# A two-layer encoder step: the first down product's weight sums moved from the feed-forward into the attention's second half

## The chip, the cores and the metric

The kernel runs on one core of a Trainium2 chip. The metric is the device time of one execution in microseconds (us). A measurement is the median of several runs. The engines are TensorE (PE, matrix products), VectorE (DVE), ScalarE (ACT), GpSimd (POOL) and SyncE (SP, which here only issues transfers).

## The reference

One inference step of a hybrid encoder with two layers, all in float32, on 1024 prompt positions and 64 sample positions (1088 together). The first layer mixes by windowed attention, the second by a complex diagonal state-space model (SSM). After each mixer comes a convolutional feed-forward:

```python
def conv_ffn(h, prev, w_up, conv_w, conv_b, w_down):
    up = h @ w_up                                   # 1024 -> 2 x 2816
    full = jnp.concatenate([prev.astype(up.dtype), up], axis=1)
    c = conv_b
    for j in range(CONV_WIDTH):                     # 3
        c = c + conv_w[j] * full[:, j:j + t]
    y = (jax.nn.gelu(c[..., :D_FF]) * c[..., D_FF:]) @ w_down   # 2816 -> 1024
    return y, full[:, -(CONV_WIDTH - 1):]
...
for i in range(DEPTH):
    mp, ... = attn_prompt(rms_norm(xp, ...), ...)   # layer 0; s5_mixer in layer 1
    xp = xp + rms_norm(mp, g_post_mix[i])
    fp, cpi = conv_ffn(rms_norm(xp, g_pre_ffn[i]), ...)
    xp = xp + rms_norm(fp, g_post_ffn[i])
```

## The kernel before

Every product is made in three fp32r matmuls of a split operand (`mm3`, L223 to L225): high weight by low activation, high by high, low by high. Weights come by `load_unit`: SyncE loads a tile `raw` (two buffers), ScalarE and VectorE split it into `whl` (L216; L193/L194 for parts of the down product). Tokens go in three blocks of 384, 384 and 320.

The stages follow one another: normalization, attention, output projection, first feed-forward, SSM, gated unit, second feed-forward.

**The attention.** `staged` (a helper) runs 34 units `scores(c, p)`, one for each chunk and half of the heads, three at a time in a pipeline: the scores (L772), maxima (L778) and exponentials (L783); the scaling (L791) and the transposes (L795); the product with the values (L802). Beside each unit it takes one step of a generator `beside()`. Its first 15 steps make the rest of K and Q, step 16 stores keys, and the next 20 make the output projection (`go`, L223 to L225, evicted at L839 and L857). So the second half of the heads runs beside the projection. At the end come the normalizations: `post_norm` (L317 to L331) and `pre_norm` (L300 to L308), which makes `hh` and `hl`, the two parts of the feed-forward's input.

**The feed-forward.** For each of 22 gate tiles, `up` makes two tiles of the up product (evicted by VectorE at L414/L416), `conv` the convolution (L422 to L424), and `gate` the gated product (L440), which SyncE stores to `gd` (L441). Twice in each gate tile, `aside()` takes a step of `ssm_prep()`, at lower priority, which prepares the SSM's matrices: first some hundred small VectorE operations (`ssm_small`), then eight chunks with matmuls `kps` (L1069), copies `kt` (L1074), transposes `wps` (L1080) and GpSimd tables `tab`.

**The down product.** For the two full blocks it is a product by Strassen's scheme in Winograd's form: seven products in place of eight, four of which read sums of weights and four sums of gate outputs. `aside()` also calls `sums(j)`, which starts and finishes these sums by a timetable `starts`: at odd steps 1 to 21 `sums_w(k)`, one for each of eleven pairs of weight tiles, and at even steps 24 to 44 `sums_g(k)` for the gate outputs. `sums_w(k)` loads 1 MB of `w_down` into `jt` (L355, SyncE), makes four VectorE operations of 128x512 in place (L358 to L361) and stores the four sums to `sd` in memory (L362, SyncE), one step later. `jt` is one tile of 12 KB per partition, taken from the pool slot `ypA` that also holds `y`, the feed-forward's output; `sums_w` uses its first 8 KB and `sums_g` (L367 to L377) its two halves in turn. The second feed-forward does the same on GpSimd's queue in a buffer `jw` of its own.

The order of instructions on each engine is made by a list scheduler that goes by priority (the order of the program) and its own cost model; `later` and `order` bend it. GpSimd's transfers take their descriptors from a scratch in SBUF, whose size is set where the program is made; before, that is the default.

Of the kernel before, what the change touches and what calls it, by code (L numbers as in the profile page):

```python
# [2 lines left out]

# [5 lines left out]
F32 = mybir.dt.float32  # L9
# [6 lines left out]
P = 128  # L16
# [10 lines left out]
SIDE = 32  # L27

PLAIN = 5

KCUT = (0, 12, 22)
GT = [[(4, "blkA")] * 3, [(4, "blkB"), (4, "blkB"), (2, "big")]]
# [2 lines left out]
KH = KF // 2  # L35
# [8 lines left out]
class Core:  # L44
    def __init__(self, ctx, tc, a):
        self.ctx, self.tc, self.nc, self.a = ctx, tc, tc.nc, a
        nc = self.nc
        pool = lambda n, **k: ctx.enter_context(tc.tile_pool(name=n, bufs=1, **k))
        self.ready, self.wsrc = [], [("w_qk", 8), ("w_qk", 0), ("w_qk", 1), ("w_v", 0), ("w_v", 1)] + [("w_qk", m) for m in (2, 3, 9, 4, 5, 6, 7)]
        self.wsrc += [("w_o", m) for m in range(KD)]  # L50
        for i in range(2):
            for m in range(KF):
                sums = [("w_sum", m, e) for e in (1, 0)] if i == 1 and m >= PLAIN else []
                self.wsrc += [("w_up", i, m)] + sums + [("w_up", i, m + KF)]
            self.wsrc += [("w_part", i, k) + x[:3] for x in PRODUCTS for k in range(0, KH, 2)]
            self.wsrc += [("w_down", i, k, mh) for c in range(2) for mh in range(2) for k in range(KCUT[c], KCUT[c + 1], 2)]
            if i == 0:
                self.wsrc.append(None)
                self.wsrc.append(None)
                self.wsrc += [("w_glu", m + e) for m in range(KD) for e in (0, KD)]  # L60
        self.const = pool("const")
        self.wts = pool("wts")
        self.blk = pool("blk")
        self.yp = pool("yp")
        self.tmp = pool("tmp")
        self.small = pool("small")
        self.open_ps()
        self.dram = pool("dr", space=bass.MemoryType.DRAM)
        jp = self.col_minus_row()
        self.ident = self.const.tile([P, P], F32, name="ident")  # L70
        nc.vector.tensor_scalar(self.ident, jp, 0.0, None, op0=ALU.is_equal)
        self.ones = self.const.tile([P, 1], F32, name="ones")
        nc.vector.memset(self.ones, 1.0 / D)
        self.eps = self.const.tile([P, 1], F32, name="eps")
        nc.vector.memset(self.eps, 1e-6)
        nc.scalar.activation(self.const.tile([P, 1], F32, name="warm"), self.eps, AF.Copy)
        pp = a["pp"]
        self.pp = self.const.tile([P, pp.shape[1]], F32, name="ppt")
        nc.sync.dma_start(self.pp[:, :64], pp[:, :64])
# [141 lines left out]
    def mm3(self, out, w, sl, xh, xl, start, stop, more=False):  # L221
# [2 lines left out]
        nc.tensor.matmul(out, w[:, 0, sl], xh, start=False, stop=False, skip_group_check=more)  # L224
        self.last_mm = nc.tensor.matmul(out, w[:, 1, sl], xh, start=False, stop=stop, skip_group_check=more)  # L225

    def fill(self, ps, n, cols, first=None):

        for _ in range(n):
            x = self.nc.tensor.matmul(ps[:, :cols], self.ident, self.pp[:, 64:64 + cols] if cols > P else self.ident[:, :cols], start=True, stop=True)  # L230
            if first is not None:
                self.order(x, first)
            first = x
        return x
# [105 lines left out]
    def ffn(self, i, h, rb, after, side=None, beside=lambda: None, x=None, g=None):  # L340

        nc, tc, a = self.nc, self.tc, self.a
# [2 lines left out]
        cb = lambda m: self.pp[:, off["cb"] + i * 44 + m:off["cb"] + i * 44 + m + 1]  # L345
        cst = self.small.tile([P, 44, 2, 2], F32, name="cst", bufs=1)
        gd = self.dram.tile([P, KF, T], F32, name=f"gd{i}")
        sd = self.sd = self.dram.tile([P, KH, 2, 2, 512], F32, name=f"sd{i}")
        td = self.dram.tile([P, KH, 2, 2, 384], F32, name=f"td{i}")

        E, Q = nc.vector, (nc.sync, nc.gpsimd)[i]

        def sums_w(k):
            x = (jt[:, :2048] if i == 0 else self.yp.tile([P, 2048], F32, name="jw", tag="ypB", bufs=1)).rearrange("p (c h m) -> p c h m", c=2, h=2)
            Q.dma_start(x, a["w_down"][i, k::KH].rearrange("c p (h m) -> p c h m", h=2))  # L355
            yield
            a11, a12, a21, a22 = x[:, 0, 0], x[:, 1, 0], x[:, 0, 1], x[:, 1, 1]
            E.tensor_add(a22, a21, a22)  # L358
            E.tensor_sub(a21, a11, a21)
            E.tensor_sub(a11, a22, a11)  # L360
            E.tensor_sub(a12, a12, a11)  # L361
            Q.dma_start(sd[:, k], x)  # L362

        def sums_g(k):
            x = jt[:, k % 2 * 1536:k % 2 * 1536 + 1536] if i == 0 else ts.tile([P, 1536], F32, name="jg", tag="t2")
            x = x.rearrange("p (c b t) -> p c b t", c=2, b=2)
            Q.dma_start(x, gd[:, k::KH, :768].rearrange("p c (b t) -> p c b t", b=2))  # L367
            yield
            a11, a12, a21, a22 = x[:, 0, 0], x[:, 0, 1], x[:, 1, 0], x[:, 1, 1]
            v = E.tensor_sub(a11, a12, a11)  # L370
            if i == 1:

                self.order(v, self.last_conv)
            E.tensor_sub(a12, a22, a12)
            E.tensor_sub(a22, a22, a11)
            E.tensor_sub(a21, a21, a22)
            Q.dma_start(td[:, k], x)  # L377


        w0 = (PLAIN + 1) * i  # L380
        starts = {2 * (k + w0) + 1: sums_w(k) for k in range(KH)}
        starts.update({2 * (k + KH) + 2: sums_g(k) for k in range(KH)})
        jobs = {}

# [42 lines left out]
        def up(ms):  # L427

            wu = {m: up_start(m) for m in ms}
            for b in range(3):  # L430
                for w, u in wu.values():
                    up_block(w, u, b)
            return {m: u for m, (w, u) in wu.items()}

        def gate(f, us):
            ta = conv(f, us.pop(f) if f in us else up([f])[f])
            nc.scalar.activation(ta, ta, AF.Gelu_apprx_tanh)
            aside()
            tb = conv(KF + f, us.pop(KF + f) if KF + f in us else up([KF + f])[KF + f])
            nc.vector.tensor_mul(ta, ta, tb)  # L440
            Q.dma_start(gd[:, f, :SEQ], ta[:, :SEQ])  # L441
            Q.dma_start(gd[:, f, SEQ:], ta[:, SEQ + 2:])
# [19 lines left out]
        def normed(bs):  # L462

            for b in bs:
                t0, n = BLK[b]
                for k in range(KD):
                    v = nc.vector.scalar_tensor_tensor(x[b][:, k], x[b][:, k], g[:, k:k + 1], rb[:, t0:t0 + n], op0=ALU.mult, op1=ALU.mult)
                    self.order(v, self.last_conv)

        def input_sums():  # L470

            V = nc.vector
            b11, b21, b12, b22 = (half(x[b], j) for b in range(2) for j in range(2))
            t1, t4 = (self.big([P, 4, 384], "t", F32) for _ in range(2))
            t2 = ts.tile([P, 4, 384], F32, name="t2", tag="t2")
            for o, u, v in ((t1, b12, b11), (b12, b22, b12), (t2, b22, t1), (t4, b21, t2)):
                for k in (slice(0, 2), slice(2, 4)):
                    self.order(V.tensor_sub(o[:, k], u[:, k], v[:, k]), self.last_conv)
            op["t1"] = [ts.tile([P, 4, 384], F32R, name=f"t1{j}") for j in range(2)]
            split(*op["t1"], t1)  # L480
            return t2, t4
# [42 lines left out]

        us = up([0, KF, 1])
        gate(0, us)
        if i == 0:
            jt = self.yp.tile([P, 3072], F32, name="jt", tag="ypA", bufs=2)
        else:
            ts_ctx = tc.tile_pool(name="ts", bufs=1)  # L530
            ts = ts_ctx.__enter__()
            op = {}
        aside()
        for f in range(1, KF):
            if i == 1 and f == 2:
                normed((0, 1))
            if i == 1 and f == 3:
                late = input_sums()
            if i == 1 and f == PLAIN - 1:
                us = up([f, KF + f])  # L540
                into_place(*late)
                normed((2,))
            if i == 1 and f >= PLAIN:
                us = seven(f, f == PLAIN)
                if f == PLAIN:
                    for j in range(2):
# [126 lines left out]
    def attention(self, h, rb, after):  # L673
        nc, tc, a = self.nc, self.tc, self.a
        off = PPO
        with tc.tile_pool(name="at", bufs=1) as ap:
# [40 lines left out]
            for tt in range(9):  # L717
# [9 lines left out]
                i = tt - 3 * b  # L727
# [135 lines left out]
            def beside():  # L863
                yield from rest()
                for p in range(2):
                    nc.gpsimd.dma_start(a["o_kp"][:, p], kT[:, p, SEQ - P:SEQ])
                    nc.gpsimd.dma_start(a["o_ks"][:, p, :64], kT[:, p, T + 64:])
                    nc.gpsimd.dma_start(a["o_ks"][:, p, 64:], kT[:, p, SEQ:T])
                yield
                yield from half()  # L870
            self.staged([scores(c, p) for p in range(2) for c in range(17)], beside())
        with self.boundary():
            for m, b in self.tail_order(KD, 4):
                if m >= 4 or b == 2:
# [732 lines left out]
```

## Time and profile before

| | us |
|---|---|
| median of 3 runs | 2242.29 (2237.78 to 2243.76) |
| the profiled execution's own time | 2249.18 |
| its span, first to last instruction | 2247.4 |
| output projection beside the scores | 207 to 314 |
| first feed-forward's gate tiles | 385 to 900 |
| `sums_w`, first operation to last | 399 to 571 |
| `sums_g` of the first feed-forward | 685 to 958 |
| granted TensorE clock, mean | 0.990 |

The profile is one execution. "Busy" is the time in which an engine executes; a matmul's end is modelled, so TensorE reads as busy while matmuls follow one another. A row of the timeline gives start, duration, engine, line, operation, output from inputs, and in brackets the idle time before it with what ended it. In the table by stretches, the number in brackets is a count of instructions.

### The profile page before, as it was taken

Reading aid. Unit: us, or ns where it says so; the run is one execution under the profiler, and the core shown is the slowest. Engines: PE = TensorE matmul, PEld = TensorE weight load, DVE = VectorE, ACT = ScalarE, POOL = GpSimd, SP = SyncE. Lnnn points to the kernel's source line nnn. Section 1 sums busy time; section 2 is a strip of 40 time slices with the busy share of each in tenths; the row PEclk is TensorE's granted clock in tenths of the full one; section 3 lists DMA queues with packets and bytes.
Section 4 is the critical chain, followed back from the end, with each engine's and each line's share of the span. In section 5 each row is a group of like instructions: output and inputs, shape, how many; then the busy total and the mean of one; then the engine's idle time right before and its main releaser. Section 6 shows DMA issues by size and latency. Waiting matters only on the chain.

```text
span 2247.4 us, 35994 instructions
## 1 busy us (share of the span) xinstructions
PE 2194.5 (98%) x13875; PEld 2121.5 (94%) x13875; DVE 1659.1 (74%) x2886; ACT 1044.5 (46%) x1890; POOL 413.9 (18%) x474
## 2 busy tenths in 40 slices
PE   9999999999999999999998899999999999999997
PEld 8987789899999999999996799999999999999997
DVE  8687648989877777667768865687977776676764
ACT  5256746422333343455534742253455445455543
POOL 5322004200042423000200034352011110110000
PEclk9999999999999999999999999999999999999999
DMA  5100015655345565887649988751266676578773
GB/s 196 37 22 29 20 62 162 239 187 207 112 136 190 174 206 176 265 292 221 224 147 339 285 277 291 266 167 65 88 213 240 235 276 224 204 264 311 223 254 99
DMA packets 208123, 428.47 MB, mean 191 GB/s; under 512 B 23312, under 2 KB 114224, under 8 KB 205008
## 3 DMA queue, kind: packets, MB, share of 16 engines
q1 hardware_dynamic: 175648, 326.56, 44.0%
q0 software_dynamic: 23984, 95.12, 11.8%
q10 hardware_dynamic: 8320, 4.49, 0.8%
q8 instruction: 109, 1.79, 0.3%
q14 instruction: 62, 0.51, 0.1%
HBM read 297.75 MB, written 128.37 MB: 190 GB/s over the span
## 4 chain that ended last, share of the span: by engine, by line
PE 45%; DMA 8%; DVE 5%; issue 2%; ACT 1%; POOL 1%; SPq 1%; DVEq 0%; ACTq 0%; POOLq 0%
PE mm L223 14%; PE mm L225 14%; PE mm L224 14%; DMA sj<-in_w_up 3%; DMA yd<-ys 1%; DMA raw<-in_w_down 1%; DMA su<-sj 1%; DMA yf<-yd 1%; DVE whl L216 1%; DMA pm<-prm 0%; DMA hd<-xs 0%; POOL sj L1389 0%; DVE wk L1304 0%; PE pr L266 0%; DMA raw<-in_w_glu 0%
## 5 line engine op out<-in xcount | busy, mean ns | idle before, releaser
L223 PE MATMUL mm<-hl,whl 128*128 128x384 f32 (+1 forms) x1960 | 643.3, 329 | 5.8 <-DVE hl L306 3.1
L224 PE MATMUL mm<-hh,whl 128*128 128x384 f32 (+1 forms) x1960 | 642.8, 328 | 0.0
L225 PE MATMUL mm<-hh,whl 128*128 128x384 f32 (+1 forms) x1960 | 640.2, 328 | 1.9 <-DVE whl L216 1.9
L223 PEld LDWEIGHTS mm<-hl,whl 128*128 128x128 f32 x1960 | 368.9, 188 | 7.6 <-DVE hl L306 4.1
L225 PEld LDWEIGHTS mm<-hh,whl 128*128 128x128 f32 x1960 | 368.6, 188 | 2.3 <-DVE whl L216 2.2
L224 PEld LDWEIGHTS mm<-hh,whl 128*128 128x128 f32 x1960 | 369.1, 188 | 0.0
L216 DVE TENSOR_TENSOR whl<-raw,whl 128x1024 fp32r<-128x1024 f32 x202 | 257.4, 1276 | 148.2 <-ACT whl L216 147.7
L216 ACT ACTIVATE whl<-raw 128x1024 fp32r<-128x1024 f32 x202 | 212.9, 1058 | 271.2 <-PE mm L225 153.9
L223 PE MATMUL mm<-gt,whl 128*128 128x384 f32 (+1 forms) x968 | 317.7, 328 | 1.4 <-ACT whl L216 1.4
L225 PE MATMUL mm<-gt,whl 128*128 128x384 f32 (+1 forms) x968 | 316.7, 328 | 0.7 <-DVE whl L216 0.7
L224 PE MATMUL mm<-gt,whl 128*128 128x384 f32 (+1 forms) x968 | 317.0, 328 | 0.0
L223 PEld LDWEIGHTS mm<-gt,whl 128*128 128x128 f32 x968 | 182.9, 189 | 1.7 <-ACT whl L216 1.7
L225 PEld LDWEIGHTS mm<-gt,whl 128*128 128x128 f32 x968 | 182.7, 189 | 1.0 <-DVE whl L216 1.0
L224 PEld LDWEIGHTS mm<-gt,whl 128*128 128x128 f32 x968 | 182.8, 189 | 0.0
L194 DVE TENSOR_TENSOR whl<-raw,whl 128x1024 fp32r<-128x1024 f32 x84 | 96.4, 1154 | 67.5 <-ACT whl L193 67.1
L193 ACT ACTIVATE whl<-raw 128x1024 fp32r<-128x1024 f32 x84 | 82.7, 988 | 107.1 <-DMA raw<-sd 46.8
L423 DVE SCALAR_TENSOR_TENSOR t<-u,ppt,t 128x1090 f32<-128x1090 f32 x88 | 123.6, 1406 | 7.4 <-ACT t L422 5.8
L424 DVE SCALAR_TENSOR_TENSOR t<-u,ppt,t 128x1090 f32<-128x1090 f32 x88 | 123.5, 1403 | 0.4
L422 ACT ACTIVATE t<-u,ppt 128x1090 f32<-128x1090 f32 x88 | 114.1, 1297 | 12.7 <-DVE t L424 5.4
L563 DVE TENSOR_TENSOR gt<-gr,gt 128x768 fp32r<-128x768 f32 (+2 forms) x106 | 90.3, 881 | 14.7 <-ACT gt L562 14.0
L562 ACT ACTIVATE gt<-gr 128x768 fp32r<-128x768 f32 (+2 forms) x106 | 78.4, 773 | 42.1 <-DMA gr<-gd 29.3
L414 DVE TENSOR_TENSOR u<-rb,mm 128x384 f32<-128x384 f32 (+1 forms) x164 | 80.4, 502 | 20.4 <-PE mm L225 15.4
(389 smaller groups left out, 4105.9 us busy)
## 6 DMA issues: line engine op xcount, KB each, us to landing
raw<-in_w_up SPq DMA_DIRECT2D x88, 512.0 KB, 4.2
raw<-in_w_down SPq DMA_DIRECT2D x74, 512.0 KB, 4.6
raw<-sd SPq DMA_DIRECT2D x40, 512.0 KB, 4.6
sj<-in_w_up POOLq DMA_DIRECT2D x68, 256.0 KB, 6.7
su<-sj POOLq DMA_DIRECT2D x34, 512.0 KB, 5.6
raw<-su SPq DMA_DIRECT2D x34, 512.0 KB, 4.5
pm<-prm SPq DMA_DIRECT2D x32, 522.0 KB, 7.7
gr<-td SPq DMA_DIRECT2D x40, 384.0 KB, 5.6
```

The lines of the kernel that those rows point to most:

```text
L193: nc.scalar.activation(w[:, 0], raw, AF.Copy)
L194: nc.vector.tensor_sub(w[:, 1], raw, w[:, 0].bitcast(F32))
L216: x = nc.scalar.activation(w[:, 0], raw, AF.Copy), nc.vector.tensor_sub(w[:, 1], raw, w[:, 0].bitcast(F32))
L223: nc.tensor.matmul(out, w[:, 0, sl], xl, start=start, stop=False, skip_group_check=more)
L224: nc.tensor.matmul(out, w[:, 0, sl], xh, start=False, stop=False, skip_group_check=more)
L225: self.last_mm = nc.tensor.matmul(out, w[:, 1, sl], xh, start=False, stop=stop, skip_group_check=more)
L414: nc.vector.tensor_mul(u[:, t0 + 2:t0 + 2 + np_], rb[:, t0:t0 + np_], ps[:, :np_])
L422: nc.scalar.activation(t, u[:, 0:T + 2], AF.Identity, bias=cb(m), scale=cw(0, m))
L423: nc.vector.scalar_tensor_tensor(t, u[:, 1:T + 3], cw(1, m), t, op0=ALU.mult, op1=ALU.add)
L424: self.last_conv = nc.vector.scalar_tensor_tensor(t, u[:, 2:T + 4], cw(2, m), t, op0=ALU.mult, op1=ALU.add)
L562: nc.scalar.activation(x[:, 0, u], raw, AF.Copy)
L563: nc.vector.tensor_sub(x[:, 1, u], raw, x[:, 0, u].bitcast(F32))
```

## The change

The eleven `sums_w` of the first feed-forward leave its timetable. A tile `jt` of 12 KB of its own is reserved for the whole run, out of `ypA`; the scratch for GpSimd's descriptors is set to 4096 bytes, which frees these 12 KB. The sums run in the attention: a generator that first idles for `FROM` = 16 steps is zipped with `beside()`, so that the first load is issued with step 17, and then each sum takes two steps: one that loads, one that adds and stores. All go through the one buffer, on SyncE's queue. `sums_g` stays where it was and uses the new tile. The second feed-forward is as before.

```diff
+FROM = 16
...
+        self.jt = pool("jt").tile([P, 3072], F32, name="jt")
...
+    def sums_w(self, i, k, x, Q):
+
+        E = self.nc.vector
+        x = x[:, :2048].rearrange("p (c h m) -> p c h m", c=2, h=2)
+        Q.dma_start(x, self.a["w_down"][i, k::KH].rearrange("c p (h m) -> p c h m", h=2))
+        yield
+        a11, a12, a21, a22 = x[:, 0, 0], x[:, 1, 0], x[:, 0, 1], x[:, 1, 1]
+        E.tensor_add(a22, a21, a22)
+        E.tensor_sub(a21, a11, a21)
+        E.tensor_sub(a11, a22, a11)
+        E.tensor_sub(a12, a12, a11)
+        Q.dma_start(self.sd[:, k], x)
+        yield
...
-        starts = {2 * (k + w0) + 1: sums_w(k) for k in range(KH)}
+        starts = {2 * (k + w0) + 1: sums_w(k) for k in range(KH)} if i else {}
...
-        if i == 0:
-            jt = self.yp.tile([P, 3072], F32, name="jt", tag="ypA", bufs=2)
-        else:
+        if i == 1:
...
-            self.staged([scores(c, p) for p in range(2) for c in range(17)], beside())
+
+            def and_sums(main):
+                self.sd = self.dram.tile([P, KH, 2, 2, 512], F32, name="sd0")
+                sums = chain(range(FROM), *(self.sums_w(0, k, self.jt, nc.sync) for k in range(KH)))
+                for _ in zip_longest(main, sums):
+                    yield
+            self.staged([scores(c, p) for p in range(2) for c in range(17)], and_sums(beside()))
...
-    nc = _bacc.Bacc("TRN2", target_bir_lowering=False, num_devices=1)
+    nc = _bacc.Bacc("TRN2", target_bir_lowering=False, num_devices=1, dynamic_dma_scratch_size=4096)
```

More of the change, by code (lines that the diff above doesn't have):

```diff
@@ L2 @@
 from contextlib import ExitStack, contextmanager
+from itertools import chain, zip_longest
 import concourse.bass as bass
@@ L347, in ffn @@
         gd = self.dram.tile([P, KF, T], F32, name=f"gd{i}")
-        sd = self.sd = self.dram.tile([P, KH, 2, 2, 512], F32, name=f"sd{i}")
+        if i:
+            self.sd = self.dram.tile([P, KH, 2, 2, 512], F32, name="sd1")
         td = self.dram.tile([P, KH, 2, 2, 384], F32, name=f"td{i}")
@@ L353, in sums_w @@
         def sums_w(k):
[L354 to L362, printed above, removed]
+            return self.sums_w(i, k, self.yp.tile([P, 2048], F32, name="jw", tag="ypB", bufs=1), Q)
         def sums_g(k):
-            x = jt[:, k % 2 * 1536:k % 2 * 1536 + 1536] if i == 0 else ts.tile([P, 1536], F32, name="jg", tag="t2")
+            x = self.jt[:, k % 2 * 1536:k % 2 * 1536 + 1536] if i == 0 else ts.tile([P, 1536], F32, name="jg", tag="t2")
             x = x.rearrange("p (c b t) -> p c b t", c=2, b=2)
```

## The prediction

> **What bounds the kernel now.** I read four views, from wide to narrow: the page's busy times, a table of busy time by stretches, the waits of TensorE, and the timelines of TensorE and VectorE around the stalls that the change can touch.
>
> The page first (engine, busy microseconds, share, instructions):
>
> ```profile
> span 2247.4 us, 35994 instructions
> PE 2194.5 (98%) x13875; PEld 2121.5 (94%) x13875; DVE 1659.1 (74%) x2886; ACT 1044.5 (46%) x1890; POOL 413.9 (18%) x474
> ```
>
> TensorE is the bound: it is idle for 2247.4 - 2194.5 = 52.9 us of the whole span. Nothing in the change takes a matmul away, so a gain can only come out of those 52.9 us, and only out of the part of them that lies where the moved work was. By stretches (busy TensorE, weight loads, VectorE, ScalarE, GpSimd):
>
> ```profile
> 120.00:160.00 40.00, 40.00 (x270) 33.15 (x269) 32.80 (x96) 22.52 (x74) 9.77 (x14) 1.00 0.10 30
> 160.00:200.00 40.00, 40.00 (x275) 33.86 (x273) 33.36 (x98) 22.72 (x69) 9.44 (x13) 1.00 0.09 27
> 207.00:307.00 100.00, 99.23 (x660) 75.08 (x657) 62.79 (x220) 67.98 (x237) 7.61 (x18) 1.00 0.08 23
> 385.00:412.00 27.00, 23.78 (x151) 22.59 (x150) 26.18 (x47) 11.76 (x24) 17.62 (x14) 1.00 0.65 226
> 430.00:445.00 15.00, 13.22 (x80) 12.96 (x79) 15.00 (x28) 5.35 (x8) 0.00 (x0) 1.00 0.49 187
> 445.00:575.00 130.00, 130.00 (x789) 130.00 (x788) 116.43 (x336) 35.77 (x52) 0.00 (x0) 1.00 0.57 200
> ```
>
> The first three rows are the attention's first and second half, the last three the start of the first feed-forward. In two short stretches, 385 to 412 and 430 to 445, VectorE is full (26.18 of 27, 15.00 of 15) and TensorE loses 27.00 - 23.78 = 3.2 and 15.00 - 13.22 = 1.8 us. From 445 to 575, where most of the moved work lies, VectorE is 90% full and TensorE loses nothing. TensorE's waits between 385 and 920, with what ended them (total, times, longest):
>
> ```profile
> PE mm L223 <- DVE hl L306: 3.1, 3, 1.6
> PE mm L223 <- DVE u L414: 1.8, 1, 1.8
> PE wps L1080 <- DVE kt L1074: 2.0, 1, 2.0
> PE wps L1080 <- DVE kt L1074: 2.4, 2, 1.4
> PE wps L1080 <- DVE w L894: 1.6, 2, 1.2
> ```
>
> All of them are ended by VectorE: 3.1 by the last normalized block of the feed-forward's input, 1.8 by an eviction, and 2.0 + 2.4 + 1.6 = 6.0 by the state-space preparation that runs beside the feed-forward. The most that the change can win in this stretch is therefore 3.1 + 1.8 + 6.0 = 10.9 us.
>
> **What the change takes out of the feed-forward.** Eleven weight sums, each one load, four VectorE operations of 128x512 and one store (durations are min/median/max; then size and time to landing):
>
> ```profile
> L358 DVE TENSOR_TENSOR jt<-jt x11: 678/692/694, 399.3 to 563.5; 128x512 f32<-128x512 f32 x11
> L361 DVE TENSOR_TENSOR jt<-jt x11: 682/684/1356, 404.8 to 570.1; 128x512 f32<-128x512 f32 x11
> jt<-in_w_down SPq DMA_DIRECT2D x11, 1024.0 KB, 5.9
> sd<-jt SPq DMA_DIRECT2D x11, 1024.0 KB, 4.1
> ```
>
> A set of four costs VectorE 4 x 0.69 = 2.76 us, all eleven 30.4 us, spread from 399 to 571. I go through the stalls one at a time. The first set lies at 399 to 406, among the last steps of the normalization; VectorE, then TensorE and ScalarE at the same place:
>
> ```profile
> 399.31 0.68 DVE L358 TENSOR_TENSOR jt<-jt 128x512 f32<-128x512 f32 x1
> 400.07 0.78 DVE L359 TENSOR_TENSOR jt<-jt 128x512 f32<-128x512 f32 x1
> 400.84 0.81 DVE L331 TENSOR_TENSOR q<-q,xl 128x640 f32<-128x640 f32 x1
> 401.58 1.49 DVE L256 TENSOR_TENSOR sqb<-sqb 128x640 f32<-128x640 f32 x1
> 402.99 0.68 DVE L360 TENSOR_TENSOR jt<-jt 128x512 f32<-128x512 f32 x1
> 403.92 1.00 DVE L306 SCALAR_TENSOR_TENSOR hl<-q,ppt,hh 128x320 fp32r<-128x320 f32 x2
> 401.69 1.02 ACT L300 ACTIVATE hh<-q,ppt 128x320 fp32r<-128x320 f32 x2 [1.60 <-DVE q L331]
> 399.45 0.41 PE L223 MATMUL mm<-hl,whl 128*128 128x320 f32 x1 [0.55 <-DVE hl L306]
> 404.51 0.41 PE L223 MATMUL mm<-hl,whl 128*128 128x320 f32 x1 [1.58 <-DVE hl L306]
> ```
>
> TensorE stands 1.58 us at 404.51 for the last hl. Ahead of that hl, VectorE ran three of the moved operations: two before L331, which ScalarE's hh waited for, and one between. Without them hl comes 0.68 + 0.78 + 0.68 = 2.1 us earlier, more than the stall: **-1.6 us**. The other two waits on hl (3.1 - 1.6 = 1.5 together) end by 399.45, when the first moved operation has only just started, and stay. The third set lies at 432:
>
> ```profile
> 432.56 0.68 DVE L358 TENSOR_TENSOR jt<-jt 128x512 f32<-128x512 f32 x1
> 433.16 1.29 DVE L440 TENSOR_TENSOR t<-t 128x1090 f32<-128x1090 f32 x1
> 434.46 0.69 DVE L359 TENSOR_TENSOR jt<-jt 128x512 f32<-128x512 f32 x1
> 435.07 1.35 DVE L423 SCALAR_TENSOR_TENSOR t<-u,ppt,t 128x1090 f32<-128x1090 f32 x1
> 436.34 0.55 DVE L414 TENSOR_TENSOR u<-rb,mm 128x384 f32<-128x384 f32 x1
> 436.94 0.44 PE L223 MATMUL mm<-hl,whl 128*128 128x384 f32 x1 [1.78 <-DVE u L414]
> ```
>
> Two moved operations stand in the unbroken VectorE queue ahead of the eviction L414 that TensorE waits for. By the starts they hold it up (433.16 - 432.56) + (435.07 - 434.46) = 1.2 us of the 1.78; if the scheduler, with a freer VectorE, also starts L440 earlier, all of it goes. I take **-1.4 us**, between -1.2 and -1.8.
>
> The other nine sets free VectorE where TensorE doesn't wait, so directly they bring 0. Indirectly they let the preparation's long run of small VectorE operations, which has the lower priority, end earlier, and with it the eight chunks that follow:
>
> ```profile
> L1080 PE MATMUL wps<-ident,w x64: 270/272/333, 616.0 to 893.6; 128*128 128x128 f32 x64
> ```
>
> Eight groups of transposes from 616 to 894, one every 39.6 us, and the five stalls of 6.0 us are in front of some of them. If the chain starts earlier, the last chunks fall clear of the crowded end, but sums of the gate outputs still lie among the others, on the same VectorE, and the change leaves them where they are. Bounds: 0 (the chunks only shift and meet the next crowded place) and -6.0. I take **-2.0 us**, a third: the last chunk's 1.2 and about one more stall; it is the weakest term. It could also be positive by some microseconds if shifted chunks meet worse places.
>
> **What it puts into the attention.** Step 17 of the work beside the scores takes the first load, each next step adds or loads, so the eleven sets start with the output projection and take two steps each:
>
> ```profile
> L223 PE MATMUL go<-ol,whl x80: 305/336/445, 207.5 to 314.2; 128*128 128x384 f32 x64, 128*128 128x320 f32 x16
> 265.56 0.16 DVE L787 TENSOR_TENSOR s<-s 128x4 f32<-128x4 f32 x1 [1.76 <-ACT s L785]
> 266.04 1.01 DVE L791 TENSOR_SCALAR ptT<-ptT,s 128x192 f32<-128x192 f32 x4
> 270.21 1.03 PE L795 MATMUL tps<-ident,ptT 128*128 128x128 f32 x8
> raw<-in_w_o SPq DMA_DIRECT2D x8, 512.0 KB, 3.4
> ```
>
> The projection's 20 steps take 314.2 - 207.5 = 107 us, 5.3 us each; a set comes every 10.7 us and adds 2.76, so VectorE goes from 63% to 63 + 26 = 89%. What hides it: VectorE stands 1.76 us in each step for ScalarE's exponentials, room for two of the four operations, and the scaled scores are ready at 267.05 while TensorE transposes them at 270.21, a lead of 3.2 us, more than one whole set. That a fuller VectorE does not reach TensorE here is seen next door: from 120 to 200 VectorE is 82 to 83% busy in the same score work and TensorE loses 0.00. 89% is a little beyond, so I take **+0.5 us**; bounds 0 and the sets' part that doesn't fit the gap, 11 x (2.76 - 1.76) = +11.0. A gain is excluded but for the 100.00 - 99.23 = 0.8 that is idle there now.
>
> On SyncE's queue each store now waits for the adds, and each next load for that store (one buffer, 4.1 us to landing), in front of the eight loads of the output projection's weights (3.4 us) and the first of the feed-forward. A projection weight serves several steps of 5.3 us and is loaded ahead; cost 0, and if that lead were gone 4.1 us once per held load, inside the +11.0 taken as the bound. In the feed-forward the same queue is relieved of 22 transfers, where no TensorE wait names a weight load: 0. The 12 KB buffer no longer takes a slot of the tile pool that holds y; TensorE doesn't wait for that slot in the waits above: 0.
>
> GpSimd's transfers now have 4096 bytes of descriptor scratch, after 12 KB are taken from it. They are thickest while the second layer's weight sums are made, 1320 to 1450:
>
> ```profile
> su<-sj POOLq DMA_DIRECT2D x32, 512.0 KB, 5.7
> sj<-in_w_up POOLq DMA_DIRECT2D x62, 256.0 KB, 6.6
> ```
>
> On average (62 x 6.6 + 32 x 5.7) / 130 = 4.5 are in flight; I take 0. [...]
>
> **Sum.** -1.6 - 1.4 - 2.0 + 0.5 = -4.5 us. The profiled execution took 2249.18 us, 1.8 more than its span and 6.9 more than the median of the three runs, 2242.29, which spread over 6 us. The sum made on the first gives 2244.7; taken from the median, **2237.8 us**, 0.20% less. I call 0.3% (6.7 us) what a measurement of this kernel can tell from no change.
>
> **Rivals.**
> *VectorE's relief never reaches TensorE.* TensorE's queue is full from 445 to 575 although VectorE is 90% busy, and small operations of the preparation may fill the freed places at 400 and 433 as well. Against it: they have the lower priority, so they should run where nothing of the main work is ready. Then 0 to -1 us: 2242. Chance 20%. [...]
> *The preparation's stalls go as well.* With VectorE free early, all eight chunks finish ahead of TensorE's turn: -1.6 - 1.8 - 6.0 = -9.4, 2232.9. For it: each of the stalls is ended by VectorE. Against: the chunk chain passes through transfers, and the gate sums stay. Chance 25%.
> *VectorE becomes the bound in the attention's second half.* A set is issued back to back, does not fit the 1.76 us gap, and ScalarE's exponentials and TensorE's transposes wait in turn. It decides from the point where a set delays a step by more than the lead of 3.2 us; its price is the +11.0 above, less the 3.0 of the two sure stalls: +8.0, 2250.3. Against it: the rows at 82 to 83%. Chance 9%.
> *The scratch throttles GpSimd's transfers.* If only one were in flight, 34 pairs would each wait a further 6.6 us and VectorE behind them: up to +220 us. 4.5 in flight against a ring of unknown depth; chance 2%.
>
> **How the numbers follow.** The forecast's own case has 44%: -4.5, within 0.3%, with some 5 of the 44 beyond -6.7 if the weakest term is larger. Faster: 0.05 + 0.23 of the preparation's case = 0.28. Same: 0.39 + 0.20 ("never reaches") + 0.02 (a preparation's case that falls short) + 0.01 (an attention's case that does) = 0.62. Slower: 0.08 + 0.02 = 0.10. The range goes from all 10.9 us of waits gone, 2231.4, to the attention's cost at half its bound with the two sure stalls gone and nothing else, 2242.3 + 5.5 - 3.0 = 2244.8, rounded out to 2231 and 2246.
>
> **What would show it.** Right: the stalls of 1.58 at 404 and 1.78 at 437 gone or under 0.6; VectorE under 85% from 445 to 575; about 89% in the attention's second half with TensorE losing under 1.5 us; the first wps group well before 616. Wrong: TensorE waits on the score operations (L778 to L791) between 207 and 326, new waits on weight loads there, GpSimd's transfers landing later than 6.6 us from 1320 to 1450, or wps stalls of more than 6 us.

## The result, and the profile after

The changed kernel takes 2276.34 us (median of 4 runs, 2273.29 to 2281.96), the kernel before beside it 2240.15 (4 runs, 2237.78 to 2243.76): a ratio of 1.0163, 95% interval 1.0134 to 1.0192. It is slower by 36 us where a gain of 4.5 was forecast. Its profiled execution took 2273.3 us.

The page's first part shows no trace of that; busy times are almost those of before:

```profile
span 2271.5 us, 35988 instructions
PE 2198.6 (97%) x13875; PEld 2122.8 (93%) x13875; DVE 1654.9 (73%) x2886; ACT 1040.5 (46%) x1890; POOL 407.2 (18%) x474
```

The first surprise is where the sums ran. The instructions on `jt` (durations min/median/max in ns, then first and last start):

```profile
L235 SPq DMA_DIRECT2D jt<-in_w_down x11: 378/379/843, 5.4 to 172.5; - x11
L238 DVE TENSOR_TENSOR jt<-jt x11: 675/691/1228, 22.3 to 178.2; 128x512 f32<-128x512 f32 x11
L242 SPq DMA_DIRECT2D sd<-jt x11: 326/327/327, 26.9 to 183.8; - x11
```

The first load is issued at 5.4 us and the last store at 183.8, before the output projection begins. The list scheduler takes whatever is ready, in the order of priority; with a tile of their own the loads wait for nothing. On SyncE's queue the first of them stands in front of three blocks of x:

```profile
5.45 0.44 SPq L235 DMA_DIRECT2D jt<-in_w_down  x1
9.80 0.34 SPq L212 DMA_DIRECT2D raw<-in_w_qk  x1
10.19 3.61 SPq L1545 DMA_DIRECT2D y<-in_x  x3
```

The issue of the three blocks begins when it did before (10.39 us there), but takes 3.61 us in place of 1.53, and blocks of their two sizes land later: 8.7 and 10.8 us after issue, in place of 7.2 and 7.8.

On VectorE the additions stand among the operations of the attention, which run in the order that the scheduler made. At 107.87 one waits 2.46 us for its load, and rotary and score operations wait behind it: L707, whose input L705 had finished at 105.41, starts at 109.21. Then TensorE waits (second fence):

```profile
104.86 0.55 DVE L705 TENSOR_TENSOR rx<-rb,mm 128x384 f32<-128x384 f32 x1
107.87 0.69 DVE L238 TENSOR_TENSOR jt<-jt 128x512 f32<-128x512 f32 x1 [2.46 <-DMA jt<-in_w_down]
...
109.21 0.59 DVE L707 STREAM_SHUFFLE rx<-rx 128x384 f32<-128x384 f32 x1
...
117.19 0.74 DVE L800 TENSOR_SCALAR ptT<-ptT,s 128x64 f32<-128x64 f32 x4
```

```profile
117.59 1.09 PE L804 MATMUL tps<-ident,ptT 128*128 128x128 f32 x4 [5.92 <-DVE ptT L800]
```

In the table by stretches, before:

```profile
0.00:40.00 40.00, 36.12 (x189) 35.25 (x190) 33.71 (x43) 24.91 (x40) 25.39 (x23) 0.91 0.68 243
80.00:120.00 40.00, 40.00 (x256) 37.95 (x255) 26.04 (x74) 12.83 (x39) 10.79 (x10) 1.00 0.09 29
```

and after, with the two stretches of the prediction (the second half of the attention is 11 us later):

```profile
0.00:40.00 40.00, 31.57 (x157) 29.40 (x158) 34.66 (x46) 24.88 (x41) 24.12 (x23) 0.91 0.77 282
80.00:120.00 40.00, 34.08 (x215) 32.83 (x214) 26.67 (x62) 9.79 (x23) 9.05 (x10) 0.93 0.52 187
218.00:318.00 100.00, 99.25 (x659) 75.09 (x656) 62.77 (x220) 67.87 (x237) 7.59 (x18) 1.00 0.08 25
445.00:575.00 130.00, 130.00 (x788) 130.00 (x787) 117.45 (x349) 38.70 (x58) 4.30 (x2) 1.00 0.25 86
```

TensorE starts 157 and 215 multiplies in place of 189 and 256. The second half, where the forecast had put the sums, is untouched (62.77 us of VectorE against 62.79). So the projection starts 10.8 us late:

```profile
L227 PE MATMUL go<-ol,whl x80: 305/336/448, 218.3 to 325.0; 128*128 128x384 f32 x64, 128*128 128x320 f32 x16
L1095 PE MATMUL wps<-ident,w x64: 270/272/476, 630.5 to 918.5; 128*128 128x128 f32 x64
```

The last `wps` is 24.9 us late (893.6 before). A second loss of 14 us thus lies between the projection's start and there, most of it in the feed-forward, where nothing but the sums was touched. TensorE's waits from 385 to 960:

```profile
PE wps L1095 <- DVE w L909: 14.3, 4, 8.1
PE wps L1095 <- DVE kt L1089: 4.8, 3, 2.5
PE mm L227 <- DVE hl L324: 1.0, 1, 1.0
PE pr L284 <- DVE sqb L278: 0.3, 1, 0.3
```

The waits on hl and on the eviction are down from 4.9 to 1.0, as forecast; those on the preparation have gone from 6.0 to 19.1.

### The profile page after: what moved, and what is told of

It is laid out like the page before. It is cut to its first block, busy times and chain, and to the rows that moved or that the text cites. A ratio compares the mean times of both kernels' runs of the same rounds, so it can differ in the third digit from the quotient of the medians.

```text
span 2271.5 us, 35988 instructions
## 1 busy us (share of the span) xinstructions
PE 2198.6 (97%) x13875; PEld 2122.8 (93%) x13875; DVE 1654.9 (73%) x2886; ACT 1040.5 (46%) x1890; POOL 407.2 (18%) x474
## 4 chain that ended last, share of the span: by engine, by line
PE 37%; DMA 13%; DVE 8%; ACT 4%; issue 2%; SPq 1%; POOL 0%; ACTq 0%; DVEq 0%; POOLq 0%
PE mm L227 9%; PE mm L229 9%; PE mm L228 9%; DMA raw<-in_w_down 4%; DMA raw<-sd 3%; PE pb L227 1%; PE pb L229 1%; PE pa L228 1%; PE pb L228 1%; PE pa L229 1%; PE pa L227 1%; DVE whl L198 1%; ACT whl L197 1%; DMA yd<-ys 1%; DMA gr<-gd 1%
## 5 line engine op out<-in xcount | busy, mean ns | idle before, releaser
L220 DVE TENSOR_TENSOR whl<-raw,whl 128x1024 fp32r<-128x1024 f32 x202 | 253.2, 1255 | 147.1 <-ACT whl L220 146.3
L198 DVE TENSOR_TENSOR whl<-raw,whl 128x1024 fp32r<-128x1024 f32 x84 | 94.6, 1133 | 78.0 <-ACT whl L197 77.6
L572 DVE TENSOR_TENSOR gt<-gr,gt 128x768 fp32r<-128x768 f32 (+2 forms) x106 | 89.9, 879 | 11.2 <-ACT gt L571 10.8
```

The lines of the kernel that those rows point to most:

```text
L198: nc.vector.tensor_sub(w[:, 1], raw, w[:, 0].bitcast(F32))
L220: x = nc.scalar.activation(w[:, 0], raw, AF.Copy), nc.vector.tensor_sub(w[:, 1], raw, w[:, 0].bitcast(F32))
L572: nc.vector.tensor_sub(x[:, 1, u], raw, x[:, 0, u].bitcast(F32))
```

## The experiments

Three questions: what the early place costs, what the loss in the feed-forward comes from, and what could be won at all. The table gives each run's median, its ratio to the kernel before on the same chip, and from its profile the start of the projection, first and last `wps`, and the wait of `wps` on w and on kt (385 to 960). The first run is also a second profile of the kernel before's order (span 2238.4).

| run | us | ratio (95%) | go | wps | w, kt |
|---|---|---|---|---|---|
| before | 2240.15 | | 207.5 | 616.0 to 893.6 | 1.6, 4.4 |
| after | 2276.34 | 1.0163 (1.0134 to 1.0192) | 218.3 | 630.5 to 918.5 | 14.3, 4.8 |
| 1 scratch | 2243.4 | 0.9999 (0.9984 to 1.0014) | 206.8 | 614.0 to 891.9 | 1.7, 4.4 |
| 2 held | 2275.1 | 1.0138 (1.0116 to 1.0159) | 207.4 | 631.3 to 921.6 | 14.8, 3.9 |
| 3 no additions | 2269.42 | 1.0116 (1.0088 to 1.0145) | 211.2 | 623.3 to 913.9 | 13.3, 5.1 |
| 4 own tile | 2256.56 | 1.0065 (1.0043 to 1.0088) | 219.9 | 625.1 to 904.1 | 2.1, 4.6 |
| 5 numbers | 2259.61 | 1.0076 (1.0056 to 1.0096) | 220.5 | 625.9 to 908.1 | 2.9, 5.9 |
| 6 held, numbers | 2259.92 | 1.0070 (1.0049 to 1.0090) | 207.4 | 623.5 to 901.8 | 1.7, 4.3 |
| 7 none | 2260.93 | 1.0083 (1.0059 to 1.0107) | 207.1 | 618.5 to 908.6 | 12.8, 5.2 |
| 8 none, numbers | 2242.48 | 0.9997 (0.9985 to 1.0009) | 207.2 | 612.7 to 891.0 | 2.6, 3.8 |
| 9 not counted | 2264.82 | 1.0094 (1.0073 to 1.0115) | 207.4 | 621.1 to 912.2 | 15.9, 4.7 |
| 10 LOW 1550 | 2257.94 | 1.0061 (1.0043 to 1.0080) | 208.2 | 620.7 to 914.9 | 0.5, 14.3 |
| 11 LOW 1450 | 2260.26 | 1.0065 (1.0046 to 1.0083) | 207.7 | 607.1 to 901.0 | 9.6, 6.0 |
| 12 wider | 2251.05 | 1.0029 (1.0018 to 1.0039) | 207.5 | 606.8 to 895.9 | 0, 6.6 |
| 13 moved, no gate additions | 2248.18 | 1.0029 (1.0017 to 1.0041) | 207.4 | 621.1 to 896.0 | 3.9, 5.3 |
| 14 no gate additions | 2254.1 | 1.0059 (1.0041 to 1.0077) | 207.1 | 614.0 to 900.4 | 8.8, 2.8 |

**1. The scratch alone**, in the kernel before.

```diff
-    nc = _bacc.Bacc("TRN2", target_bir_lowering=False, num_devices=1)
+    nc = _bacc.Bacc("TRN2", target_bir_lowering=False, num_devices=1, dynamic_dma_scratch_size=4096)
```

> The kernel before with one edit: the scratch for generated transfer descriptors is 4 KB; no sums are moved and no tile is added. Theory 'early sums' (the 36 us come from the sums running in the kernel's first 190 us): within 0.3% of before, 2234 to 2246 us, and the waits of before unchanged. Rival 'scratch' (the smaller scratch holds back GpSimd's and generated transfers): 2250 us or more, with POOL's share or its transfers' landing times longer.

No difference: the scratch is out.

**2. The sums held back** to the second half.

```diff
+        if i == 0:
+            self.order(ld, self.loaded)
...
+            self.order(v, self.last_nm)
```

> The kernel after with the sums held back to where the prediction took them to run: the first set's load is ordered behind the weight load issued last on its queue, its last addition behind the score operation issued last. Nothing is left out. Theory 'early sums': the 10.8 us lost before the output projection come back (its first multiply at 207 to 209 us instead of 218.3), and with them what follows from it: 2234 to 2250 us. Rival 'the feed-forward lost its filler' (taking the sums out of the first feed-forward, not their early place, makes the preparation's products wait longer): the start comes back but the wait of wps on w (L909) stays near 14 us, 2250 to 2266 us. Third theory 'attention' (the additions hold up the scores wherever they run in it): the output projection begins at 212 us or later.

The edit orders the first of a set's four operations, and the other three need its data or its place. The additions run from 214 to 356 us and the projection starts on time, but the whole is as slow as after: the wait on w stays at 14.8. The early place is not the only cause. And the forecast's own place isn't free: between 207 and 307 TensorE starts 639 multiplies (660 and 656 in the two profiles of the old order), with VectorE at 77% in place of 63.

**3. Loads and stores without the additions.**

```diff
-        E.tensor_add(a22, a21, a22)
...
+        if i:
+            E.tensor_add(a22, a21, a22)
...
```

> The kernel after without the four additions and subtractions of each of the first layer's eleven sets (the loads and stores stay, so the first down product multiplies unsummed weights): 44 VectorE operations of about 0.7 us less, some 30 us of VectorE in the first 190 us and its waits for the loads. If VectorE (its work and its waiting at the head of the queue for a set's load) makes the early loss: the output projection begins at 207 to 211 us. If the transfers make it (22 MB of loads and stores beside x and w_qk): it still begins at 214 us or later. Either way the loss in the feed-forward tells whether it hangs on the start.

The projection is late by 3.7 to 4.4 us (against the two profiles of before) instead of 10.8 to 11.5: by subtraction, the transfers make about a third of the early loss, VectorE's work and waiting the rest. The wait on w is not touched by it.

**4. Only the tile**: the sums stay in the feed-forward's timetable, in a `jt` of their own.

```diff
+        self.jt = pool("jt").tile([P, 3072], F32, name="jt")
...
-            jt = self.yp.tile([P, 3072], F32, name="jt", tag="ypA", bufs=2)
```

> The kernel before with a tile of its own for the sums (and the 4 KB scratch that makes room for it); the sums stay in the first feed-forward's timetable, so the attention's program is untouched. Theory 'the slot was the gate' (what kept the sums late was the buffer shared with the attention's q, not the place in the program): their first load starts by 10 us as in after, and the time is after's within 0.5%, 2265 to 2288 us. Rival 'the place in the program': the first load starts after 330 us and the time is 2230 to 2246 us.

Half right. The first load starts at 5.4 and the last at 175.6, as in after, so the shared slot was what held the sums back, and the projection is 12 to 13 us late. But the time is 0.65% over before, not 1.6%, since the feed-forward loses nothing. The sums run just as early as in after, so the second loss doesn't come from when they run.

**5 and 6. The numbers.** An instruction takes the next priority number when the program is written, and a lower number goes first. `ssm_prep` is scheduled `LOW` = 1500 priority numbers behind its place. Each `sums_w` takes 6 numbers, a step of the feed-forward about 87 otherwise. With 66 taken out, 1500 numbers reach half a step further; in TensorE's order, as the traces give it, 3891 multiplies stand ahead of the first `wps` in after and 3853 in before (38 fewer); ahead of the last chunk's there are 5528 in both. These two add the numbers back and nothing else, to after and to run 2.

```diff
+            if i == 0 and 1 <= j <= 2 * KH:
+                self.tc.cur_priority += (5, 1)[j % 2]
```

> The kernel after, with the priority counter moved on by hand in the first feed-forward by the numbers that the eleven sets used to take there (1 at a step that starts a set, 5 at a step that ends one, 66 in all); not one instruction is added or left out. Theory 'priority numbers' (the preparation is placed 1500 numbers behind its place in the program; with 66 numbers fewer in the feed-forward's first half it falls some 50 numbers, half a step, later at first and not at all at the end, so its eight chunks are pressed together): wps waits on w for under 3 us instead of 14.3, the down product starts about 12 us after the kernel before's instead of 25, and the time is that of the run with an own tile, 2250 to 2262 us. Rival 'less to fill with' (the sums' absence itself starves or shifts the preparation): the wait of 14 us stays and the time is 2270 to 2282 us.

> The kernel with the sums held beside the output projection, and with the same 66 numbers added in the feed-forward. Theory: both losses are gone; what is left are the waits of some 7 us that the sums make in the attention's end (3.3 on sqa, 1.7 and 1.0 on ol, 1.2 on ptT) less the 3.4 us of stalls that go at the feed-forward's start: 2238 to 2250 us, between 0 and 6 us over before. Rival 'less to fill with': 2255 us or more. If the prediction's own sum holds (its only mistake was when the sums run): 2233 to 2238 us.

The wait on w falls to 2.9 and 1.7, and 15 to 17 us go (by the medians; 0.7 to 0.9% by the ratios). Run 6 misses its range: with the projection on time and the preparation in place it is still 0.7% over before. The time alone would suit its rival (2255 or more), but the wait on w, which 'less to fill with' would keep, is gone. Some 9 us are lost between the projection's start and the first `wps` (623.5 against 614.0), with waits like these of TensorE (215 to 470):

```profile
PE pr L288 <- DVE sqa L282: 3.2, 1, 3.2
PE mm L227 <- DVE hl L328: 1.8, 1, 1.8
PE go L227 <- DVE ol L841: 1.7, 1, 1.7
PE tps L810 <- DVE ptT L806: 1.2, 2, 0.8
```

From 207 to 470 the granted clock is 0.97 in run 6 and 1.00 in run 1, and TensorE starts 1583 multiplies in place of 1634. The rest of the 0.7%, some 7 us, lies behind the last `wps` and is not explained.

**7 and 8. No sums at all**, without and with their numbers; the first down product reads plain weights in their place.

```diff
-        starts = {2 * (k + w0) + 1: sums_w(k) for k in range(KH)}
+        starts = {2 * (k + w0) + 1: sums_w(k) for k in range(KH)} if i else {}
```

> The kernel before with the first layer's eleven sets left out altogether, loads, additions and stores; the first down product reads plain weights in the place of the sums, in tiles of the same size. Theory 'priority numbers': though it does less, it is slower than before, by 8 to 20 us (2248 to 2262), with wps waiting on w for 10 us or more. Rival 'early or misplaced work' (every loss comes from where the sums run): 2228 to 2240 us.

> The same without the sums, with the 66 numbers added. It shows the most that could be won by taking the sums out of the feed-forward. Theory and the prediction's terms (1.6, 1.4 and 2.0 us of stalls, bounds 3 to 9): 2231 to 2239 us, and 10 to 25 us below the run without sums and without the added numbers. Rival: no difference between the two.

Leaving the work out makes the kernel slower by 0.8%, unless its numbers stay. With them it equals before. So as long as the preparation keeps its places, taking the sums out wins nothing that can be measured, and no new place for them can win by that. Another place for the preparation, with the sums out, was not run.

**9. The kernel before, its sums not counted**: whole and in place.

```diff
+            if i == 0 and 1 <= j <= 2 * KH:
+                self.tc.cur_priority -= (5, 1)[j % 2]
```

> The kernel before, whole and with its sums in their old place, except that the eleven sets take no priority numbers in the feed-forward (the counter is put back by 1 and 5 after each step). TensorE's program then has the preparation's products in the very places that the kernel after has them. Theory 'priority numbers': this alone costs what the second loss costs, 2250 to 2266 us with wps waiting on w for 10 us or more. Rival (the numbers matter only together with the missing work): 2236 to 2246 us.

Numbers alone cost 0.94%. With the 0.65% of run 4 that makes 1.59%, and the whole change costs 1.63%. One wait, in the timelines of VectorE, ScalarE and TensorE:

```profile
841.00 1.35 DVE L426 SCALAR_TENSOR_TENSOR t<-u,ppt,t 128x1090 f32<-128x1090 f32 x1
850.12 0.76 DVE L1045 TENSOR_TENSOR ct<-m 128x576 f32<-128x576 f32 x1 [7.77 <-DMA raw<-in_w_up]
...
862.05 0.56 DVE L370 TENSOR_TENSOR jt<-jt 128x384 f32<-128x384 f32 x1 [3.67 <-DMA jt<-gd]
...
869.20 0.68 DVE L896 TENSOR_TENSOR w<-m 128x512 f32<-128x512 f32 x1
```

```profile
848.09 2.00 ACT L1104 ACTIVATE tp<-tl 128x1024 f32<-128x1024 f32 x1 [8.44 <-DMA tl<-kd]
```

```profile
869.93 1.12 PE L1082 MATMUL wps<-ident,w 128*128 128x128 f32 x4 [9.96 <-DVE w L896]
```

VectorE isn't short of time: it stands 7.77 us in front of a preparation step and 3.67 in front of a gate sum, and w is behind both. The row puts the 7.77 down to a weight load, which this step does not read. ScalarE's `tp` fits better: it waited 8.44 us for a load of its own and ended at 850.09, and four other waits in front of this step (17.3 us in all) are put down to it.

**10 to 12. Other places for the preparation**, in the kernel before: `LOW = 1550`, `LOW = 1450`, and 3 numbers more at each of the steps 1 to 22.

> The kernel before with the preparation placed 1550 numbers behind in place of 1500: all its chunks come later, the first by 34 multiplies of TensorE's program and the last by 48, so that they are not pressed together. If the wait of wps on w comes from the pressing (38 multiplies fewer, some 6 us, for the same eight chunks): 2238 to 2248 us, the waits near the 6 us of before. If it comes from where a chunk's VectorE operations stand against the gate sums (each set's load and additions at fixed steps): 2250 us or more, waits over 12 us.

> The kernel before with the preparation 1450 numbers behind: all chunks earlier by 48 multiplies, none pressed (the last one too). By 'pressing': 2238 to 2246 us, no change over 0.2%. By 'place against the gate sums': a change either way of 5 us or more, 2228 to 2260 us.

> The kernel before with 66 numbers more in the first half of the feed-forward (3 at each of 22 steps): the first chunk comes 49 multiplies earlier, the last where it was, so that the chunks lie 240 multiplies apart in place of 232. By 'pressing' this is the opposite of the kernel after, and takes from the 6 us of waits on kt and w: 2233 to 2241 us, wps waiting under 4 us. If the first chunk comes too early for the small operations that go ahead of it: a new wait of 3 us or more on kt or w of the first chunk, 2242 to 2250 us.

Every move loses, later or earlier, pressed or not: 'pressing' falls, the place counts. Run 12, meant to gain, is 0.3% slower; neither of its expectations holds, since its longest wait (3.4 on kt) ends at 773, far behind the first chunk. In all three the sums are as before, so they can't be the cause. No run of the study beats the kernel before.

**13 and 14. Without the gate sums' additions**, in run 9's places and in before's.

```diff
-            v = E.tensor_sub(a11, a12, a11)
...
+            else:
+                self.tc.cur_priority += 4
```

> The kernel before without priority numbers for the weight sums (the preparation in the places that the kernel after has), and without the four additions of each of the first layer's eleven gate sums (their loads and stores and their priority numbers stay; the down product so multiplies unsummed gate outputs). If the moved chunks wait because they stand behind these additions on VectorE's queue: the wait of wps on w falls from 15.9 to under 5 us and the time is 2236 to 2248 us. If the preparation's own chain (its buffers, its transfers, ScalarE) makes the wait: it stays over 10 us, 2255 to 2265 us.

> The same additions left out of the kernel before with its own places: the measure for the run beside it. 2230 to 2243 us, waits of wps on kt and w of 6 us or less. If the additions cost the unmoved kernel as much as the moved one, this comes 10 us or more below before, and the difference between the two runs is what the move alone costs.

In the moved places the wait on w falls from 15.9 to 3.9, as it would if w stood behind these additions. But in the old places it rises from 1.6 to 8.8 without them, and run 14, expected at 2230 to 2243, is 0.6% slower than before. Leaving them out does more than free their time, so the two runs don't show that they made the wait. No single operation has a fixed price here. That the number sets the place, and the place the wait, is shown; which step of the preparation's chain makes a place good is open.

## Why the prediction was wrong

**Two steps failed.** The first is "Step 17 of the work beside the scores takes the first load ... so the eleven sets start with the output projection". The step sets a priority, not a time. Beside it failed "The 12 KB buffer no longer takes a slot ...: 0". I asked whether TensorE waits for that slot; I should have asked what waits for it, which was the sums' first load (390.9 us before, 5.4 with an own tile in run 4). Price: 10.8 us in place of 0. This step alone does not make the miss: run 2 puts the sums where it wanted them and is still 1.38% over before. The second is the term of the preparation, below.

**The attention, +0.5** (0 to 11): not tested by the change itself. Run 6 puts it near 9 us, close to the bound, though with an order of its own that holds the sets back. They took 142 us there, not 107, with VectorE at 78% and not 89, and so ran on into the normalization. The lead of 3.2 us covered neither the projection's ol nor that.

**The two stalls, -1.6 and -1.4**: in after they are gone but for 1.0 on hl. Yet the second was no property of the kernel: run 1's profile, of the same order, has no wait on an eviction there. And run 8, without any sums, has 1.0 us less of TensorE's waits from 385 to 960 than run 1 (8.7 against 9.7): what is won at hl (3.1 to 1.0) comes back as 1.0 on the norm of a block (nvsqb) and 0.3 in the preparation. The rival "VectorE's relief never reaches TensorE" describes that run.

**The preparation, -2.0** (0 to -6.0), is the second failed step and the larger one: the sign was wrong, +13.1 in waits (6.0 to 19.1). "It could also be positive by some microseconds if shifted chunks meet worse places" was the right mechanism and stayed outside the sum and the range. I took "starts earlier" from a freer VectorE, and left out that 66 numbers fewer move the preparation in the program. That alone costs 0.94% (run 9). The first `wps` came at 630.5, 3.7 us more than the projection's delay and 38 multiplies later in TensorE's order.

**The check on VectorE**, under 85% from 445 to 575, failed: 117.45 of 130 is 90%, and 87% from 456 to 586, where the same part of the program runs; other work moved in. **The scratch at 0** was right. No run shows how many transfers it can hold; with the 4 KB alone the kernel takes 0.9999 of before (run 1).

What stays open: of the 33.1 us between after and run 1 (spans), 11.5 lie ahead of the projection, 15.1 from there to the last `wps` (26.6 - 11.5), and 6.5 behind it, in the down product and the second layer's start. There two profiles of the old order differ by 7.3 us themselves (1353.8 and 1346.5 us from the last `wps` to the end), with a granted clock of 0.97 and 0.99 from 960 to 1400, so I put it down to nothing.

## What to carry to other kernels

Under a list scheduler a buffer that is shared by accident can be what keeps work late: before giving a tile its own memory, ask whose slot held it back. Where priorities are counted in instructions, taking instructions out moves everything that is placed by an offset; hold the count and test the two apart. And measure the ceiling first, with the work simply left out and its count held: here that run (8) would have shown that nothing was to be won.

## What the runs showed of the hardware

In the rows below, a wait cost more than itself where TensorE's granted clock dropped behind it. The granted clock is the figure behind POOL's count. In after, the first row holds the end of a wait of 1.75 us on w, the second the end of the longest, 8.05 us:

```profile
788.00:798.00 10.00, 8.24 (x51) 7.96 (x50) 9.93 (x14) 3.41 (x8) 7.51 (x4) 1.00 0.38 138
874.00:884.00 10.00, 7.92 (x40) 7.89 (x41) 8.16 (x14) 4.07 (x8) 5.00 (x4) 0.73 0.41 154
884.00:894.00 10.00, 10.00 (x63) 10.00 (x62) 5.58 (x9) 2.42 (x4) 6.77 (x6) 1.00 0.61 191
```

Around the long wait's end the clock is 0.73 and 40 multiplies run in 7.92 busy microseconds, in the next ten 63; by the timeline, multiplies of 128x384 start 0.32 us apart there up to 879.23, and 0.17 to 0.18 from 879.45 on. By the short one the clock stays at 1.00. Length alone does not decide. The next two rows follow two waits of 2.34 and 2.50 us in after (the second ended at 752.64) and a single one of 2.00 us in run 9 (ended at 780.80); the clock is 0.50 behind both:

```profile
753.00:756.00 3.00, 3.00 (x12) 3.00 (x11) 2.57 (x3) 2.09 (x3) 2.31 (x2) 0.50 0.68 263
781.00:784.00 3.00, 3.00 (x12) 2.77 (x12) 3.00 (x8) 2.25 (x6) 3.00 (x2) 0.50 0.63 262
```

Behind a wait of 2.12 us in after (ended at 829.88) it is 1.00 from 830 to 835. What decides is not shown. I had counted waits at their own length.

With the scratch of 4 KB the landing times of GpSimd's transfers for the second layer's weight sums were not longer: over the whole run, the 68 loads of 256 KB (`sj`) land in 6.4 us in after and 6.3 in run 1, 6.7 before; the 34 stores of 512 KB (`su`) in 5.5 and 5.6, 5.6 before.
